# Moving one gate tile of layer 0 behind its queries, and dealing out the filler beside its attention

## The chip, the cores and the metric

The kernel runs on one core of one Trainium2 chip. The metric is device time in microseconds (us) of one launch. Before the change three runs took 1505.15, 1508.58 and 1509.13 us, a median of 1508.58 us. The engines are called by their names in the profile: PE multiplies matrices, ACT, DVE and POOL work on vectors, SP issues most of the transfers. Each engine takes its instructions strictly in the order of its own queue.

## What is computed

Two layers of a backbone over 512 latent tokens and 256 context tokens, 1024 channels wide, in float32. Of a layer only this matters here:

```python
h = modulate(rmsnorm(x, norm1_g[l]), shift, scale)        # shift, scale, gates: silu(cond) @ w_mod[l] + b_mod[l]
z = h @ w_in[l]                                           # columns: q 512 | k 128 | v 128 | u 512 | g 512
attn = softmax(rope(rmsnorm(q)) @ rope(rmsnorm(k)).T) @ v # context sees context, latent sees all 768 keys
gm = gelu(u) * (w_s @ group_layernorm(gelu(g)) + b_s)     # 4 groups of 128 channels, 128x128 position mixing
x = x + gate1 * (concat(attn, gm) @ w_out[l])
x = x + gate2 * (square(relu(modulate(rmsnorm(x, norm2_g[l])) @ w_ff1[l])) @ w_ff2[l])
```

## The kernel before

**Precision.** A product in float32 precision is three matmuls: every operand is kept as a rounded part `hi` and a rest `lo`, and hi\*hi, hi\*lo and lo\*hi are summed in PSUM. A weight block of 128x1024 is loaded by SP into one of two `raw` buffers; ACT casts it to `hi` and DVE or POOL subtracts to get `lo` (`split`, L206 to L208). Blocks of `w_mod` are loaded as they are, two to a place, and multiply in plain float32. All of them pass through a ring of four places (`hi` and `lo`, `RING = 4`), filled in the order of `block_order` (L120) and freed when the last matmul that reads a block is done.

**Projection of layer 0 (L764 to L783).** `PLAN` lists the pieces in order. `kv`, `A0` to `A2` and `B0` to `B2` are banks: 256 tokens by 256 columns, 48 matmuls of 256 columns into a PSUM buffer `pb` (two of them). A bank of A or B is two groups of `g`: it goes through gelu, the layer norm on DVE, the mixing matmuls with `w_s`, and then POOL multiplies the gate tile by it (L760). `u0` to `u3`, in the table `u2`, `u3` and the split pieces `w0`, `x0`, `w1`, `x1`, are the gate tiles: 128 channels of `u` by 768 tokens, for a whole tile two halves of 24 matmuls of 384 columns into a buffer `pa` (two of them), each half followed by ACT, DVE, ACT, DVE for gelu (`gelu2`, L690). The gate tile is written to `U` (tiles `C0`, `C1`), and the mixing of its group multiplies it in place. Behind the plan come the queries (L779 to L783): two groups of 256 columns by three banks of 256 tokens. DVE normalizes and turns a bank of queries (`qk`, L604), ACT and POOL split it (`stack`, L628), PE transposes it (`turn`, L636).

**Attention of layer 0 (L832 to L915).** There are 48 tiles of 128 queries of one head: 16 of the context (256 keys), then 32 of the latent tokens (768 keys). A tile is two products with the keys into `pa`, a row maximum on DVE (L842), an exponential on ACT (L845), transposes of the probabilities on PE (L861) with a copy on ACT and a subtraction on DVE (L863, L864), and for two tiles together the product with the values (L882 and before). Behind every tile `Flow.step` takes one piece of other work for PE, a filler, from a list.

**Fillers of layer 0.** First come four pieces of `w_mod` (letter m below; a piece is four float32 matmuls of 512 columns that use 32 columns of the array), then the string `FILL0` mixes 16 pieces `o` (one block row of `w_out` times the gMLP half of the mix, 12 matmuls of 384 columns) with 12 pieces m, then 8 pieces of the context's attention half of `w_out`, 12 matmuls of 256 columns each. `make_gm` (L786), which runs ahead of the first `o`, splits the four finished groups of `U` into `hi` and `lo`: ACT casts (L791), DVE subtracts for groups 0 and 1, POOL for groups 2 and 3 (L792). All four are needed within the first piece `o`.

**Order.** The program text gives an order, with a virtual clock (`fl.vt`) that puts off the later halves of a tile; the scheduler of the tile framework then sets the order on each engine. The rows in fences below are taken from that order. A name such as `pa_2029` is a buffer of the pool `pa`; `S` is the silu of the conditions, `A_39` to `A_46` the input `h`.

Of the kernel before, what the change touches and what calls it, by code (L numbers as in the profile page):

```python
# [12 lines left out]
ALU = mybir.AluOpType  # L13
# [14 lines left out]
PK1 = {"c": (0, 8), "cc": (8, 16), "bmod": (16, 112), "ng": (112, 144), "gn": (144, 152), "ident": (152, 280), "sel": (280, 312)}  # L28
PK2 = {"qg": (0, 64), "kg": (64, 128), "bs": (128, 640)}

PAR = {"KF": 1, "XO": 1, "MS": 3, "KB": 6, "S0": 200.0, "S2": 1.0, "BK": 1, "CS": 0, "S1": 2400.0, "NS": 2, "CX": 0,
# [14 lines left out]
class Flow:  # L48
# [59 lines left out]
    def run_fillers(self):  # L108
# [2 lines left out]

FILL0 = "oooooooomomomomomomomomommmm"
EARLY = [f"A{i}" for i in range(7, 3, -1)] + [f"B{i}" for i in range(7)] + ["C0", "C1"] + [f"A{i}" for i in range(7, 3, -1)]
PLAN = (("w0", "w1", "x0", "kv", "A0", "u2", "A1", "A2", "u3", "x1", "B0", "B1", "B2"),
        ("u0", "u3", "A0", "A1", "kv", "u1", "u2", "B0", "B1"))


def block_order():  # L120
# [3 lines left out]
    for l in range(DEPTH):  # L124
# [4 lines left out]
        for s in PLAN[l]:  # L129
            if s[0] in "uw":  # L130
                o.append(("u", l, int(s[1])))
            elif s in ("A0", "B0"):
                o += tok(l, 3 if s == "A0" else 4)
        o += tok(l, 1) + tok(l, 2)
        if l == 0:
            o += mod(4) + mod(5)
            rest = mod(6) + mod(7) + mod(8) + mod(9) + mod(10) + mod(11)
            n = 0
            for c in FILL0:
                if c == "m":  # L140
                    o.append(rest.pop(0))
                else:
                    if n % 4 == 0:
                        o.append(("out", 0, 0, n // 4))
                    n += 1
            o += rest
        else:
            o += [("out", l, 0, nb) for nb in range(4)]
# [12 lines left out]
def trunk(ctx: ExitStack, tc: tile.TileContext, xT, pk1, pk2, rope, wsT, w_mod, w_tok, w_u, w_out, w_ff1, w_ff2, outT):  # L161
# [431 lines left out]
    def layer(l, h, nxt, K, kv=None, kv0=0):  # L593
# [120 lines left out]
        def u_tile(m):  # L714
            wb = take("u", l, m)
            ps = pb() if nd == 1 and m < 2 else pa()
            for i, (off, n) in enumerate(dense):
                fm_mms(ps[:, i * 512:i * 512 + n], w8(wb, h), off, n)
                if i == nd - 1:
                    release()  # L720
                fl.tick()
                gelu2(U[m // 2][:, m % 2, off:off + n], ps[:, i * 512:i * 512 + n], [128, n])

        mixes = []

        def sink_g(gp):
            def f(tp, ps):
# [16 lines left out]
                @once  # L744
                def mixing():
                    mx = pt((128, 2, 256))
                    for g in range(2):
                        for t in range(2):
                            c = slice(t * 256 + g * 128, t * 256 + g * 128 + 128)
                            w = slice((gp * 2 + g) * 128, (gp * 2 + g) * 128 + 128)  # L750
                            for i, (a, b) in enumerate(((0, 0), (0, 1), (1, 0))):
                                mm(mx[:, g, t * 128:t * 128 + 128], vg[:, a, c], ws[:, b, w], i == 0, i == 2, 128)
                    e = tsm([128, 2, 256])
                    for g in range(2):
                        G_ = gp * 2 + g
                        vec.scalar_tensor_tensor(out=e[:, g, :].rearrange("p (t q) -> p t q", t=2), in0=mx[:, g, :].rearrange("p (t q) -> p t q", t=2),
                                                 scalar=gnh[:, G_:G_ + 1], in1=P2("bs")[:, G_ * 128:G_ * 128 + 128].unsqueeze(1).broadcast_to([128, 2, 128]),
                                                 op0=ALU.mult, op1=ALU.add)
                    u = U[gp][:, :, tp * 256:tp * 256 + 256]
                    pool_e.tensor_tensor(out=u, in0=e, in1=u, op=ALU.mult)  # L760
                mixes.append(mixing)
                fl.defer(PAR["G%d" % l], mixing)
            return f
# [15 lines left out]
        with region('q%d' % l):  # L779
            for g in range(2):  # L780
                qp = TokProj(l, 1 + g, h, NP, sink_q(g))
                for tp in range(NP):
                    qp.bank(tp)  # L783

        GM = []

# [133 lines left out]

        def mixed(a, b):
            for c in FILL0:
                next(a if c == "o" else b)
                yield
            yield from a
            yield from b

# [252 lines left out]
```

## Time and profile before

| | |
|---|---|
| three runs | 1505.15, 1508.58, 1509.13 us |
| the profiled execution | 1511.25 us, of which the span from the first to the last instruction is 1509.5 us |
| mean granted clock of PE | 0.991 |
| busy share of the span | PE 97%, DVE 60%, ACT 42%, POOL 23% |
| layer 0, projection and queries | about 40 to 176.5 us of the span |
| layer 0, attention | about 176.5 to 348 us |

A group's row in the profile gives the line, the engine, the operation, what it writes and reads, its shape and count, then busy time and mean duration in ns, then the idle time of the engine in front of it and who ended that. A timeline row gives start and duration in us. Matmuls overlap, so PE's pace is read from the distance of starts or from the chain of waits, not from the mean duration of one.

### The profile page before, as it was taken

Reading aid. Unit: us, or ns where it says so; the run is one execution under the profiler, and the core shown is the slowest. Engines: PE = TensorE matmul, PEld = TensorE weight load, DVE = VectorE, ACT = ScalarE, POOL = GpSimd, SP = SyncE. Lnnn points to the kernel's source line nnn. Section 1 sums busy time; section 2 is a strip of 40 time slices with the busy share of each in tenths; the row PEclk is TensorE's granted clock in tenths of the full one; section 3 lists DMA queues with packets and bytes.
Section 4 is the critical chain, followed back from the end, with each engine's and each line's share of the span. In section 5 each row is a group of like instructions: output and inputs, shape, how many; then the busy total and the mean of one; then the engine's idle time right before and its main releaser. Section 6 shows DMA issues by size and latency. Waiting matters only on the chain.

```text
span 1509.5 us, 22333 instructions
## 1 busy us (share of the span) xinstructions
PE 1459.7 (97%) x8770; PEld 1288.2 (85%) x8770; DVE 903.9 (60%) x1667; ACT 640.4 (42%) x1078; POOL 342.6 (23%) x322
## 2 busy tenths in 40 slices
PE   6999799999999999999999999999999999999998
PEld 2899787797889899998989888997889888888887
DVE  5877967787755555444444436766887544444443
ACT  3543355674545353433334233536774333322221
POOL 0112421312045552322323213146212000000000
PEclk9999999999999999999999999999999999999999
DMA  9121344401234333333333311221001333333222
GB/s 364 64 71 57 112 168 170 140 1 43 63 109 134 118 112 126 112 125 100 126 111 126 106 49 57 84 84 58 29 1 56 112 98 98 98 98 98 97 94 75
DMA packets 49945, 148.80 MB, mean 99 GB/s; under 512 B 5424, under 2 KB 6832, under 8 KB 49840
## 3 DMA queue, kind: packets, MB, share of 16 engines
q1 hardware_dynamic: 49264, 146.46, 29.5%
q8 instruction: 69, 1.13, 0.3%
q10 hardware_dynamic: 576, 0.92, 0.2%
q14 instruction: 36, 0.29, 0.1%
HBM read 145.26 MB, written 2.10 MB: 98 GB/s over the span
## 4 chain that ended last, share of the span: by engine, by line
PE 83%; DVE 8%; ACT 2%; POOL 2%; DMA 2%; issue 2%; SPq 0%; POOLq 0%; ACTq 0%; DVEq 0%
PE pa L203 52%; PE pb L203 24%; PE pt L861 3%; PE pt L203 2%; PE pb L338 1%; DMA B<-in_w_mod 1%; DMA X<-in_xT 1%; PE pt L643 1%; POOL acc L444 1%; DMA A<-in_w_mod 1%; DVE A L478 1%; DVE s L482 1%; DVE X L801 1%; DVE B L978 1%; DVE lo L208 0%
## 5 line engine op out<-in xcount | busy, mean ns | idle before, releaser
L203 PE MATMUL pa<-A,hi 128*128 128x384 f32 (+2 forms) x1696 | 449.2, 347 | 1.6 <-ACT w L971 0.7
L207 ACT CAST hi<-raw 128x1024 fp32r<-128x1024 f32 x171 | 179.5, 1051 | 466.2 <-PE pa L203 383.3
L208 DVE TENSOR_TENSOR lo<-raw,hi 128x1024 fp32r<-128x1024 f32 x155 | 194.3, 1254 | 232.8 <-ACT hi L207 229.4
L203 PEld LDWEIGHTS pa<-A,hi 128*128 128x128 f32 x1696 | 304.4, 188 | 25.7 <-ACT w L971 2.0
L203 PE MATMUL pa<-A,lo 128*128 128x384 f32 (+2 forms) x848 | 293.5, 346 | 1.1 <-DVE lo L208 1.1
L203 PE MATMUL pa<-B,hi 128*128 128x512 f32 (+1 forms) x900 | 239.8, 355 | 3.6 <-DVE X L801 3.6
L382 POOL TENSOR_TENSOR C<-C,s 128x512 f32<-128x512 f32 x112 | 164.7, 1485 | 315.5 <-ACT s L381 273.5
L203 PEld LDWEIGHTS pa<-B,hi 128*128 128x128 f32 x900 | 158.7, 189 | 31.6 <-DVE X L801 5.9
L203 PEld LDWEIGHTS pa<-A,lo 128*128 128x128 f32 x848 | 159.4, 188 | 12.2 <-DVE lo L208 1.5
L801 DVE SCALAR_TENSOR_TENSOR X<-pa,modT,X 128x512 f32<-128x512 f32 x126 | 82.9, 660 | 142.9 <-PE pa L203 142.9
L203 PE MATMUL pb<-B,hi 128*128 128x512 f32 (+1 forms) x600 | 157.9, 351 | 3.9 <-DVE X L801 3.9
L203 PE MATMUL pa<-B,lo 128*128 128x512 f32 (+1 forms) x450 | 157.7, 355 | 0.0
L203 PE MATMUL pb<-hi,A 128*128 128x256 f32 x672 | 126.4, 285 | 0.0
L203 PEld LDWEIGHTS pb<-B,hi 128*128 128x128 f32 x600 | 104.9, 191 | 18.3 <-DVE X L801 5.1
L801 DVE SCALAR_TENSOR_TENSOR X<-pb,modT,X 128x512 f32<-128x512 f32 (+3 forms) x116 | 70.9, 618 | 82.3 <-PE pb L203 82.0
L203 PEld LDWEIGHTS pb<-hi,A 128*128 128x128 f32 x672 | 106.3, 191 | 0.2 <-PE pb L203 0.2
L203 PE MATMUL pb<-B,lo 128*128 128x512 f32 (+1 forms) x300 | 104.9, 350 | 0.0
L203 PE MATMUL pb<-lo,A 128*128 128x256 f32 x336 | 95.1, 283 | 0.0
L381 ACT ACTIVATE s<-k,silu 128x512 f32<-128x512 f32 x112 | 77.0, 716 | 42.0 <-DMA k<-in_w_mod 29.0
L203 PEld LDWEIGHTS pa<-B,lo 128*128 128x128 f32 x450 | 84.1, 189 | 11.4
L203 PE MATMUL pb<-A,hi 128*128 128x512 f32 (+2 forms) x288 | 82.5, 363 | 2.2 <-POOL A L792 2.1
L864 DVE TENSOR_TENSOR A<-pt,A 128x384 fp32r<-128x384 f32 (+1 forms) x144 | 73.0, 534 | 10.2 <-ACT A L863 8.8
(173 smaller groups left out, 2224.4 us busy)
## 6 DMA issues: line engine op xcount, KB each, us to landing
raw<-in_w_ff SPq DMA_DIRECT2D x128, 512.0 KB, 3.5
k<-in_w_mod SPq DMA_DIRECT2D x96, 256.0 KB, 3.1
raw<-in_w_tok SPq DMA_DIRECT2D x19, 512.0 KB, 3.5
raw<-in_w_out SPq DMA_DIRECT2D x16, 512.0 KB, 3.4
lo<-in_w_mod SPq DMA_DIRECT2D x16, 512.0 KB, 4.5
hi<-in_w_mod SPq DMA_DIRECT2D x16, 512.0 KB, 3.7
A<-in_w_mod SPq DMA_DIRECT2D x8, 512.0 KB, 9.7
raw<-in_w_u SPq DMA_DIRECT2D x8, 512.0 KB, 3.4
```

Source lines behind the costliest of these rows:

```text
L203: pe.matmul(out, a, b, start=start, stop=stop)
L207: act.copy(hi, src)
L208: (eng or vec).tensor_tensor(out=lo, in0=src, in1=hi.bitcast(F32), op=ALU.subtract)
L338: pe.matmul(ps[q:q + 32, :], S32[:, k, :], ws_[k2 // 2][:, k2 % 2 * 512:(k2 % 2 + 1) * 512], start=k < ns, stop=k >= KT - ns)
L381: act.activation(p, w, AF.Copy, scale=s)
L382: pool_e.tensor_tensor(out=a, in0=a, in1=p, op=ALU.add)
L444: eng.tensor_tensor(out=self.acc, in0=self.acc, in1=sq, op=ALU.add)
L478: (pool_e if k % 2 < PAR['LP'].get('%d%d%d' % (l, w, off // 256), 0) else vec).scalar_tensor_tensor(out=h[k][:, 1, off:off + n], in0=t, sc ...
L482: vec.scalar_tensor_tensor(out=t, in0=xk(k)[:, off:off + n], scalar=Amod[l][w][:, k, cond:cond + 1], in1=self.bc[:, 0:n], op0=ALU.mult, op ...
L801: vec.scalar_tensor_tensor(out=xs, in0=src[:, s - off:e - off], scalar=modT[l][:, i * 8 + m, cond:cond + 1], in1=xs, op0=ALU.mult, op1=ALU ...
L861: pe.transpose(tp_[:, (kt - k0) * 128:(kt - k0) * 128 + 128], p[:, kt * 128:kt * 128 + 128], ident)
L864: vec.tensor_tensor(out=ptl[:, k0:k0 + step, d], in0=src, in1=pth[:, k0:k0 + step, d].bitcast(F32), op=ALU.subtract)
```

## The change

Layer 0's gate tile 3 is taken out of `PLAN` and multiplied behind the last bank of the queries (`LATE`, `u_tile`); its weight block moves in `block_order` to behind the two blocks of each group of queries. The mixing of group 3 now runs ahead of it: DVE writes the mixed values of that group straight into `U`, POOL multiplies only the other group of the pair, and when the tile is there, gelu writes to a scratch tile and POOL multiplies `U` by that, in two halves of 384 columns (new line 731). `FILL0` begins with two pieces m instead of the `o`s, has five dots, and the generator answers a dot with "wait": behind that tile of attention there is no filler. The 16 `o` and 12 `m` stay. Layer 1 has `LATE` None and stays as it is. Behind the change line numbers are 5 to 19 higher.

```diff
--- before.py
+++ after.py
@@ -28,6 +28,9 @@
 PK1 = {"c": (0, 8), "cc": (8, 16), "bmod": (16, 112), "ng": (112, 144), "gn": (144, 152), "ident": (152, 280), "sel": (280, 312)}
 PK2 = {"qg": (0, 64), "kg": (64, 128), "bs": (128, 640)}
 
+LATE = (3, None)
 
 
 PAR = {"KF": 1, "XO": 1, "MS": 3, "KB": 6, "S0": 200.0, "S2": 1.0, "BK": 1, "CS": 0, "S1": 2400.0, "NS": 2, "CX": 0,
@@ -111,9 +114,9 @@
 
 
 
-FILL0 = "oooooooomomomomomomomomommmm"
+FILL0 = "mmoooooooomomom.mom.mom.mom.mo.oo"
 EARLY = [f"A{i}" for i in range(7, 3, -1)] + [f"B{i}" for i in range(7)] + ["C0", "C1"] + [f"A{i}" for i in range(7, 3, -1)]
-PLAN = (("w0", "w1", "x0", "kv", "A0", "u2", "A1", "A2", "u3", "x1", "B0", "B1", "B2"),
+PLAN = (("w0", "w1", "x0", "kv", "A0", "u2", "A1", "A2", "x1", "B0", "B1", "B2"),
         ("u0", "u3", "A0", "A1", "kv", "u1", "u2", "B0", "B1"))
 
 
@@ -132,6 +135,8 @@
             elif s in ("A0", "B0"):
                 o += tok(l, 3 if s == "A0" else 4)
         o += tok(l, 1) + tok(l, 2)
+        if LATE[l] is not None:
+            o.append(("u", l, LATE[l]))
         if l == 0:
             o += mod(4) + mod(5)
             rest = mod(6) + mod(7) + mod(8) + mod(9) + mod(10) + mod(11)
@@ -139,7 +144,7 @@
             for c in FILL0:
                 if c == "m":
                     o.append(rest.pop(0))
-                else:
+                elif c == "o":
                     if n % 4 == 0:
                         o.append(("out", 0, 0, n // 4))
                     n += 1
@@ -719,7 +724,13 @@
                 if i == nd - 1:
                     release()
                 fl.tick()
-                gelu2(U[m // 2][:, m % 2, off:off + n], ps[:, i * 512:i * 512 + n], [128, n])
+                u, src = U[m // 2][:, m % 2, off:off + n], ps[:, i * 512:i * 512 + n]
+                if m == LATE[l]:
+                    v = gelu2(None, src, [128, n])
+                    pool_e.tensor_tensor(out=u, in0=v, in1=u, op=ALU.mult)
+                else:
+                    gelu2(u, src, [128, n])
 
         mixes = []
 
@@ -750,14 +761,17 @@
                             w = slice((gp * 2 + g) * 128, (gp * 2 + g) * 128 + 128)
                             for i, (a, b) in enumerate(((0, 0), (0, 1), (1, 0))):
                                 mm(mx[:, g, t * 128:t * 128 + 128], vg[:, a, c], ws[:, b, w], i == 0, i == 2, 128)
+                    u = U[gp][:, :, tp * 256:tp * 256 + 256]
                     e = tsm([128, 2, 256])
                     for g in range(2):
                         G_ = gp * 2 + g
-                        vec.scalar_tensor_tensor(out=e[:, g, :].rearrange("p (t q) -> p t q", t=2), in0=mx[:, g, :].rearrange("p (t q) -> p t q", t=2),
+                        to = u if G_ == LATE[l] else e
+                        vec.scalar_tensor_tensor(out=to[:, g, :].rearrange("p (t q) -> p t q", t=2), in0=mx[:, g, :].rearrange("p (t q) -> p t q", t=2),
                                                  scalar=gnh[:, G_:G_ + 1], in1=P2("bs")[:, G_ * 128:G_ * 128 + 128].unsqueeze(1).broadcast_to([128, 2, 128]),
                                                  op0=ALU.mult, op1=ALU.add)
-                    u = U[gp][:, :, tp * 256:tp * 256 + 256]
-                    pool_e.tensor_tensor(out=u, in0=e, in1=u, op=ALU.mult)
+                    gs = [g for g in range(2) if gp * 2 + g != LATE[l]]
+                    gs = slice(gs[0], gs[-1] + 1)
+                    pool_e.tensor_tensor(out=u[:, gs], in0=e[:, gs], in1=u[:, gs], op=ALU.mult)
                 mixes.append(mixing)
                 fl.defer(PAR["G%d" % l], mixing)
             return f
@@ -781,6 +795,8 @@
                 qp = TokProj(l, 1 + g, h, NP, sink_q(g))
                 for tp in range(NP):
                     qp.bank(tp)
+            if LATE[l] is not None:
+                u_tile(LATE[l])
 
         GM = []
 
@@ -920,8 +936,11 @@
 
         def mixed(a, b):
             for c in FILL0:
-                next(a if c == "o" else b)
-                yield
+                if c == ".":
+                    yield "wait"
+                else:
+                    next(a if c == "o" else b)
+                    yield
             yield from a
             yield from b
 

```

PE at the end of the queries. Before, the last bank of queries (`pb_2008`) is followed by the first tile's products (`pa_2092`), the first pieces of `w_mod` (L338, into `pb_2104` and `pb_2185`) and the transposes of queries (L643):

```order
L203 MATMUL pa_2092<-B_108_493,B_249_1617 128x256
L338 MATMUL pb_2104<-hi_1859,S_88 32x512 x2
L338 MATMUL pb_2104<-lo_1860,S_88 32x512 x2
L643 MATMUL pt_2109<-c_70,k_2045 128x128 x4
L643 MATMUL pt_2115<-c_70,k_2045 128x128 x4
L203 MATMUL pa_2128<-B_107_492,B_249_1617 128x256
L203 MATMUL pa_2128<-B_108_493,B_249_1617 128x256
L338 MATMUL pb_2104<-hi_1863,S_88 32x512 x2
L338 MATMUL pb_2104<-lo_1864,S_88 32x512 x2
L338 MATMUL pb_2185<-hi_2146,S_88 32x512 x2
L338 MATMUL pb_2185<-lo_2147,S_88 32x512 x2
```

Now half of gate tile 3 (`pa_2029`) stands between the last bank and those; here is the end of that half and what follows, down to the start of the other half:

```order
L208 MATMUL pa_2029<-A_46_178,hi_1796 128x384 x2
L208 MATMUL pa_2029<-A_46_178,lo_1797 128x384
L648 MATMUL pt_2054<-c_70,k_1982 128x128 x4
L648 MATMUL pt_2060<-c_70,k_1982 128x128 x4
L208 MATMUL pa_2125<-B_107_492,B_243_1552 128x256
L208 MATMUL pa_2125<-B_108_493,B_243_1552 128x256
L343 MATMUL pb_2137<-hi_1800,S_88 32x512 x2
L343 MATMUL pb_2137<-lo_1801,S_88 32x512 x2
L343 MATMUL pb_2137<-hi_2066,S_88 32x512
L648 MATMUL pt_2107<-c_70,k_2074 128x128 x2
L208 MATMUL pa_2029<-A_39_171,hi_1796 128x384 x2
```

What moved: the 48 matmuls of the gate tile now stand in front of the first and the second tile of attention, the second half of them behind transposes that read `k_2074`, which POOL writes.

DVE at the same place. Before, the subtractions of `make_gm` (L792) stand between two banks of queries, ahead of the operations that read the last bank `pb_2008` (L610 reads ACT's square of it):

```order
L297 SCALAR_TENSOR_TENSOR m_1995<-m_1997,m_1995 128x8
L625 TENSOR_TENSOR w_1988<-w_1988,m_1995 128x512
L792 TENSOR_TENSOR A_381_2274<-C_124_571,A_381_2274 128x768
L792 TENSOR_TENSOR A_382_2277<-C_124_571,A_382_2277 128x768
L610 TENSOR_REDUCE m_2074<-s_2072 128x8
L622 TENSOR_TENSOR w_2076<-pb_2008,k_33_148 128x512
```

Now the last bank is done (L630 is what was L625) when gelu of the gate tile comes (L698, L702 on `pa_2029`), the first tile's maximum (L858) among it, and `make_gm` (L808) stands behind the first half:

```order
L630 TENSOR_TENSOR w_2013<-w_2013,m_2016 128x512
L698 SCALAR_TENSOR_TENSOR s_2077<-s_2077,pa_2029 128x384
L582 TENSOR_SCALAR k_982_4820<-k_982_4820 128x64 x2
L592 TENSOR_SCALAR k_982_4820<-k_982_4820 128x512
L858 TENSOR_REDUCE m_2128<-pa_2125 128x1
L702 SCALAR_TENSOR_TENSOR s_2077<-s_2077,pa_2029 128x384
L863 RECIPROCAL m_2133<-m_2131 128x1
L808 TENSOR_TENSOR A_407_2358<-C_124_571,A_407_2358 128x768
L808 TENSOR_TENSOR A_408_2361<-C_124_571,A_408_2361 128x768
L698 SCALAR_TENSOR_TENSOR s_2119<-s_2119,pa_2029 128x384
L858 TENSOR_REDUCE m_2155<-pa_2152 128x1
L351 STREAM_TRANSPOSE s_2168<-pb_2137 128x512
```

What moved: `make_gm` on DVE went from ahead of the last bank of queries to behind it, and from then on maxima of attention tiles alternate with the gate tile's gelu.

POOL at the same place. Before, `make_gm` (L792) and the `lo` parts of two blocks of `w_out` stand in one run:

```order
L631 TENSOR_TENSOR k_2045<-w_1900,k_2045 128x8x64
L792 TENSOR_TENSOR A_383_2280<-C_125_572,A_383_2280 128x768
L792 TENSOR_TENSOR A_384_2283<-C_125_572,A_384_2283 128x768
L208 TENSOR_TENSOR lo_2157<-raw_2154,hi_2156 128x1024
L208 TENSOR_TENSOR lo_2163<-raw_2160,hi_2162 128x1024
L631 TENSOR_TENSOR k_2166<-w_1988,k_2166 128x8x64
L850 COPY rc_2102<-m_2100 128x64
```

Now the two multiplies of the gate tile (L731) are there, and `make_gm` for the last group (`A_410`) stands behind both blocks of `w_out` and four copies of the attention tiles' reciprocals (L866):

```order
L636 TENSOR_TENSOR k_2074<-w_1925,k_2074 128x8x64
L731 TENSOR_TENSOR C_125_572<-s_2077,C_125_572 128x384
L866 COPY rc_2135<-m_2133 128x64
L808 TENSOR_TENSOR A_409_2364<-C_125_572,A_409_2364 128x768
L636 TENSOR_TENSOR k_2142<-w_2013,k_2142 128x8x64
L731 TENSOR_TENSOR C_125_572<-s_2119,C_125_572 128x384
L866 COPY rc_2162<-m_2160 128x64
L213 TENSOR_TENSOR lo_2248<-raw_2245,hi_2247 128x1024
L866 COPY rc_2135<-m_2183 128x64
L213 TENSOR_TENSOR lo_2254<-raw_2251,hi_2253 128x1024
L866 COPY rc_2162<-m_2224 128x64
L808 TENSOR_TENSOR A_410_2367<-C_125_572,A_410_2367 128x768
```

What moved: the last operand that the first piece `o` needs is now written at the end of this run, not at its start.

## Prediction

> **What bounds the kernel now.** The page comes first: how much of the span each engine is busy.
>
> ```profile
> span 1509.5 us, 22333 instructions
> PE 1459.7 (97%) x8770; PEld 1288.2 (85%) x8770; DVE 903.9 (60%) x1667; ACT 640.4 (42%) x1078; POOL 342.6 (23%) x322
> ```
>
> PE is the bound, and the change takes no matmul away. It can gain only where PE stands or runs slowly, so the next view is the table of busy time by stretch, laid over layer 0 from the first banks of `g` to the end of attention (columns: stretch, its length, busy time of PE, weight loads, DVE, ACT, POOL with counts, granted clock, DMA share, GB/s).
>
> ```profile
> 97.00:145.00 48.00, 47.63 (x379) 47.49 (x379) 38.66 (x137) 17.15 (x26) 10.36 (x8) 1.00 0.22 67
> 145.00:176.50 31.50, 31.09 (x261) 30.71 (x261) 28.96 (x84) 10.89 (x19) 9.22 (x7) 1.00 0.21 69
> 176.50:195.50 19.00, 10.52 (x62) 4.00 (x62) 16.29 (x26) 6.58 (x14) 11.30 (x7) 0.73 0.56 198
> 230.00:290.00 60.00, 59.91 (x442) 46.70 (x440) 45.54 (x102) 35.77 (x79) 11.56 (x20) 1.00 0.49 167
> 290.00:324.00 34.00, 32.67 (x264) 31.11 (x261) 27.61 (x58) 23.11 (x53) 10.55 (x17) 1.00 0.10 32
> 324.00:348.00 24.00, 20.81 (x137) 18.12 (x136) 19.36 (x43) 17.36 (x41) 1.89 (x8) 0.93 0.00 1
> ```
>
> Two stretches fall out, with clocks of 0.73 and 0.93: the end of the queries (176.5 to 195.5) and the last tiles of attention (324 to 348). In the first, the timeline of PE shows the stop, and a finer table of stretches the clock behind it.
>
> ```profile
> 176.77 0.62 PE L338 MATMUL pb<-hi,S 128*32 128x512 f32 x2
> 177.77 1.09 PE L643 MATMUL pt<-c,k 128*128 128x128 f32 x8
> 178.62 0.48 PE L203 MATMUL pa<-B,B 128*128 128x256 f32 x2
> 179.49 0.60 PE L338 MATMUL pb<-lo,S 128*32 128x512 f32 x2
> 187.94 1.07 PE L338 MATMUL pb<-hi,S 128*32 128x512 f32 x2 [7.85 <-DVE w L622]
> 188.80 1.07 PE L338 MATMUL pb<-hi,S 128*32 128x512 f32 x2
> 188.00:192.00 4.00, 4.00 (x13) 1.00 (x14) 3.33 (x14) 1.07 (x3) 1.19 (x1) 0.50 0.31 84
> ```
>
> PE waits 7.85 us for a `pb` buffer that DVE has not read, and then works at a clock of 0.50. DVE's and POOL's timelines say why.
>
> ```profile
> 178.38 2.28 DVE L625 TENSOR_TENSOR w<-w,m 128x512 f32<-128x512 f32 x1
> 180.59 6.11 DVE L792 TENSOR_TENSOR A<-C,A 128x768 fp32r<-128x768 f32 x2
> 187.21 0.68 DVE L622 TENSOR_TENSOR w<-pb,k 128x512 f32<-128x512 f32 x1
> 176.50 3.61 POOL L792 TENSOR_TENSOR A<-C,A 128x768 fp32r<-128x768 f32 x2 [1.48 <-ACT A L791]
> 180.08 5.80 POOL L208 TENSOR_TENSOR lo<-raw,hi 128x1024 fp32r<-128x1024 f32 x2
> ```
>
> The read of the last bank (L622) stands behind two operations of `make_gm` of 3.05 us each.
>
> **Prices.** From the chain of waits, 24 matmuls of 384 columns (half of the gate tile), 36 of 256 and 24 of 512; then groups from the projection's stretch, the queries' and the last tiles'.
>
> ```profile
> 110.49 4.43 PE pa L203 x24
> 97.11 4.38 PE pb L203 x36
> 1192.45 5.44 PE pa L203 x24
> L693 DVE SCALAR_TENSOR_TENSOR s<-s,pa 128x384 f32<-128x384 f32 x2 | 1.1, 534 | 0.0
> L697 DVE SCALAR_TENSOR_TENSOR C<-s,pa 128x384 f32<-128x384 f32 x2 | 1.1, 546 | 0.0
> L692 ACT ACTIVATE s<-pa 128x384 f32<-128x384 f32 x2 | 1.0, 486 | 2.0 <-PE pa L203 2.0
> L630 ACT CAST k<-w 128x512 fp32r<-128x512 f32 x4 | 2.5, 627 | 7.1 <-DVE w L625 7.1
> L644 ACT CAST B<-pt 128x512 fp32r<-128x512 f32 x6 | 3.3, 590 | 4.5 <-PE pt L643 4.5
> L631 POOL TENSOR_TENSOR k<-w,k 128x512 fp32r<-128x512 f32 x4 | 5.4, 1339 | 13.0 <-ACT k L630 13.0
> L608 ACT ACTIVATE s<-pb 128x512 f32<-128x512 f32 x4 | 2.4, 597 | 7.4 <-PE pb L203 7.4
> L610 DVE TENSOR_REDUCE m<-s 128x8 f32<-128x512 f32 x5 | 3.4, 680 | 1.2 <-ACT s L608 1.2
> L614 DVE TENSOR_TENSOR w<-pb,G 128x512 f32<-128x512 f32 x4 | 2.7, 680 | 0.0
> L618 DVE TENSOR_TENSOR s<-pb,G 128x256 f32<-128x256 f32 x8 | 3.0, 413 | 0.0
> raw<-in_w_u SPq DMA_DIRECT2D x8, 512.0 KB, 3.4
> hi<-in_w_mod SPq DMA_DIRECT2D x5, 512.0 KB, 4.6
> L203 PE MATMUL pb<-A,B 128*128 128x256 f32 x49 | 9.8, 326 | 0.2 <-ACT A L863 0.2
> L861 PE MATMUL pt<-c,w 128*128 128x128 f32 x54 | 9.3, 293 | 2.8 <-DVE A L864 2.8
> L203 PE MATMUL pa<-B,B 128*128 128x512 f32 x14 | 5.3, 438 | 0.2 <-ACT w L845 0.2
> L203 PE MATMUL pa<-B,B 128*128 128x256 f32 x14 | 2.8, 281 | 0.0
> PE pt L861 <- DVE A L864: 2.8, 6, 1.3
> ```
>
> So a 256-column matmul costs 0.122 us, one of 512 columns 0.227; eight transposes take 178.62 - 177.77 = 0.85, 0.106 each; a float32 matmul of a piece m is 0.25 at full clock (four between the starts at 176.77 and 177.77). The moved tile is 2 x 4.43 = 8.9 us of PE.
>
> **Part A, the end of the queries.** What PE does in 176.5 to 195.5 would take at full clock 4 x 1.0 (four groups of L338) + 0.85 + 8 x 0.122 (four tiles' products) + 4 x 0.106 and some 0.3 of small ones = 6.5 us. 19.0 - 6.5 = 12.5 us are lost there. The change takes the cause away: `make_gm` on DVE is behind the last bank, and the tile's 8.9 us stand where PE stood. What is late next, counted from T, the end of the last bank of queries:
>
> First, `pt_2107`, in front of the tile's second half, needs `k_2074` from POOL. PE reaches it at T + 4.43 + 0.85 + 0.24 + 5 x 0.25 = 6.8. ACT casts for it behind the square of the first half and two casts of transposed queries: the transposes end at T + 5.3, then 2 x 0.59 + 0.63, then POOL 1.34, T + 8.4. PE waits 1.6.
>
> Second, there are now six pieces m behind the first six tiles instead of four, each two loads of 512 KB, and the gate tile's block holds one of four places till its last matmul, at T + 12.8. The piece loaded into that place (`hi_2186`) lands 4.6 later by the row above, T + 17.4; PE reaches it after six transposes, two products, seven matmuls of m and two transposes, 2.9 us on: T + 15.7. PE waits 1.7.
>
> Third, maxima of the first tiles stand behind gelu and `make_gm` on DVE, and the first piece `o` behind POOL's last part of `make_gm`. The bounds are 0, if all is covered, and 6.1, if `make_gm` stops PE for the 6.11 that it takes now; I take 2.2, nearer to the low end, since these maxima no longer hold a `pb` buffer. Together PE loses 5.5 us, between 3.3 and 9.4. Gain A: 12.5 - 5.5 = 7.0 us.
>
> At which clock would those waits leave PE? The row 290:324 holds one wait, and keeps 1.00; the row 324:348 shows 0.93 with six waits on one subtraction. Waits of 1.6 and 1.7 us, 8 us apart, are nearer to the first: no charge, and 24 x 0.07 = 1.7 us as the other bound. The Trainium skill (TensorE: Matmul & The Clock Gate, Part 1) says that the clock is halved after an idle window of about 3.4 us and restored after a busy one; the stretch at 0.50 behind a wait of 7.85 us agrees, and by that rule the charge would be 0.
>
> POOL gets two more reads of SBUF right there, beside DVE's L808. The Trainium skill (SBUF — State Buffer, Who interferes with whom) states that GpSimd reading SBUF and a DVE operation with two SBUF inputs exclude each other for a whole instruction, which speaks against this place; L625's 2.28 us while POOL's L792 runs agree, against 0.68 of L622 at the same width when POOL is done. By it only L808 would pay, the maxima and L880, with one SBUF input at most, would not, and the third wait above would be about 1 us smaller.
>
> **Part B, the projection.** Without the tile PE has 79.5 - 8.9 = 70.6 us of work from 97 to 176.5. DVE was busy 38.66 + 28.96 = 67.6; the tile's gelu, 2 x (0.53 + 0.55) = 2.2, goes, so 65.4 remain: 93% of PE's time instead of 85%. DVE idled 11.9 us in them, and 5.2 are left. Bounds: 0, if its two PSUM buffers absorb it, and 6.7, if it idles as much as before. PE idled 0.37 + 0.41 = 0.8 us in these stretches so far, so I take 1.0, with 4, nearer to the low bound, as the upper end. The tile's block is loaded behind the queries' four on SP, in 3.4 us, and its cast and subtraction move into the queries' stretch; three banks still lie between them and T, which hides both, and a load that came late would stop PE at T for what it lacks.
>
> **Part C, the attention tiles.** Before, 4 + 28 + 8 pieces stand behind the first 40 of 48 tiles, and the last eight have none. Work in 324 to 348: 49 x 0.122 + 54 x 0.106 + 14 x 0.227 + 14 x 0.122 for the same products' 256 columns + about 0.9 of small rows = 17.5 us, so 6.5 of the 24.0 are lost, 0.8 a tile. Now 4 + 33 + 8 = 45 tiles pass through the list, five of them by a dot. Five bare tiles at the end get work: 5 x 0.8 = 4.1 us. Five earlier tiles go bare; between filled neighbours such a tile costs between 0 and 0.8, and I take 0.3, as 230 to 290 runs with DVE at 76%. Gain C: 4.1 - 1.5 = 2.6, between 0 and 4.1. The last tile's own tail, with most of the low clock, stays.
>
> **Sum.** The tile's 8.9 us leave one stretch and come back in another: 0. Then -7.0 + 1.0 - 2.6 = -8.6 us. The span of 1509.5 becomes 1500.9. The profiled execution took 1511.25, 1.75 outside its span, and is 2.67 above the median of the runs, 1508.58; against that median the forecast is 1508.58 - 8.6 = 1500.0 us. The ends: -9.2 - 4.1 = -13.3, 1495.3; and -3.1 + 4 + 1.7 = +2.6, 1511.2.
>
> **Rivals.**
>
> 1. *The wait moves instead of going.* `A_410`, which the first `o` needs, now stands on POOL behind two blocks of `w_out` and four copies of attention tiles, and PE takes nothing past that `o`. If POOL comes 5 us after PE there, part A keeps 2.0, and the sum is -2.0 + 1.0 - 2.6 = -3.6: 1505.0. For it: POOL's L208 took 2.90 us each beside DVE. Against: six m, six tiles and 8.9 us stand in front.
> 2. *DVE becomes the bound of the projection.* All its 11.9 us of idling stay: 65.4 + 11.9 = 77.3 against 70.6, +6.7 us; the same lag reaches gelu and the first tiles, so that A's waits are 5.5 + 6.7 = 12.2 and its gain 0.3, and C's dots meet a DVE with no slack: 0. Sum +6.4: 1515.0, slower. It decides once DVE is more than about 3 us behind a finished bank (the next bank takes PE 48 x 0.122 = 5.9 us, and reading one takes 0.60 + 0.68 + 0.68 + 2 x 0.41 = 2.8). For it: 93% busy. Against: PE idled only 0.8 us in 79.5.
> 3. *Bare tiles are DVE's anyway.* Five dots cost 0.8 each, and fillers at the end only share PE's wait: C is +1.5 to +4.1. With 4.1: -7.0 + 1.0 + 4.1 = -1.9: 1506.7.
> 4. That the change does not do what it says is ruled out: the orders show the tile, `make_gm` and the pieces in their new places.
>
> **Chances.** About 0.3%, 4.5 us, can be told from no change, so faster means under 1504.1. Forecast 0.72 (nearly all of it faster), rival 1 0.14 (a fifth of it faster, the rest the same), rival 2 0.07 (slower), rival 3 0.07 (the same). Faster 0.73, same 0.20, slower 0.07. The range keeps the forecast's low end, rounded to 1495.0, and goes up to 1507.0, past rivals 1 and 3.
>
> **What would show it.** Right: behind the last bank no wait of PE over 3 us, a clock of 1.00 or nearly through T + 20, short waits on POOL's L636 and on a load of `w_mod`; the projection shorter by 8 us or more up to T; the bare stretch at the end of attention reduced to three tiles. Wrong: PE waiting for DVE inside the banks of `g` and the queries; a wait of over 5 us at the first `o` on POOL's L808; waits on L880 at the dots.

## The result, and the profile after

The changed kernel takes 1500.0 us (median of 6 runs, 1498.95 to 1502.22), and the kernel before beside it 1508.86 (6 runs): a ratio of 0.995, with a 95% interval of 0.9939 to 0.996 (the two medians alone divide to 0.994). The profiled execution took 1502.22 us, with a span of 1500.4, 9.1 shorter than before's. First the page's head, then the table by stretch, cut at the same places of the program as for before: the last bank of queries now ends at 168.7 instead of 176.4, and the last eight tiles of attention fill 316 to 340 instead of 324 to 348. The last row runs from that bank to the first matmul of the latent out-projection.

```profile
span 1500.4 us, 22327 instructions
```

```profile
97.00:145.00 48.00, 47.17 (x398) 47.00 (x398) 41.67 (x153) 15.58 (x24) 12.31 (x10) 1.00 0.19 62
145.00:168.70 23.70, 23.70 (x202) 23.70 (x201) 21.52 (x65) 8.36 (x15) 6.04 (x5) 1.00 0.21 70
168.70:195.50 26.80, 24.82 (x163) 15.74 (x162) 14.94 (x44) 16.36 (x37) 13.90 (x13) 1.00 0.73 254
316.00:340.00 24.00, 22.10 (x172) 20.51 (x170) 19.19 (x44) 17.28 (x42) 3.82 (x10) 1.00 0.01 2
168.70:340.20 171.50, 167.57 (x1174) 136.97 (x1173) 123.90 (x294) 106.53 (x245) 42.42 (x68) 1.00 0.36 124
```

Both bad clocks are gone: 0.73 and 0.93 have become 1.00. In the projection DVE is busy 41.67 + 21.52 = 63.2 of 71.7 us, and PE misses 0.8, as before. The last row has a counterpart in before:

```profile
176.40:347.80 171.40, 158.31 (x1126) 130.13 (x1125) 130.73 (x292) 102.20 (x239) 42.17 (x66) 0.96 0.34 118
```

Both take 171.4 or 171.5 us, but after has the gate tile in it (48 matmuls, 1174 against 1126), which starts at 168.71 and takes 4.17 us for its first half of 24 matmuls, from the first to the next instruction: 8.3 us for both at that pace. So attention gained 8.2 us and the projection lost nothing by giving the tile away. The waits of PE from 160 to 345 (what waited, for whom: sum, times, longest):

```profile
PE pt L877 <- DVE A L880: 1.3, 2, 1.0
PE pa L208 <- DVE s L702: 0.8, 1, 0.8
PE pb L343 <- DVE s L351: 0.6, 1, 0.6
PE pb L208 <- ACT A L879: 0.6, 2, 0.4
PE pt L648 <- POOL k L636: 0.5, 1, 0.5
```

The wait of 7.85 us has gone, none over 1.0 is left. There is no row for a load, and none for L808 of `make_gm`. The second and the last row stand around the gate tile's second half, in PE's timeline:

```profile
176.50 0.44 PE L648 MATMUL pt<-c,k 128*128 128x128 f32 x2 [0.52 <-POOL k L636]
177.79 0.62 PE L208 MATMUL pa<-A,hi 128*128 128x384 f32 x2 [0.84 <-DVE s L702]
```

The waits come to 3.8 us, and yet more is lost. The next table is worked out from PE's timeline: the distance between the starts of two neighbouring matmuls, less what it is at full speed (0.109 us at 128 columns, 0.120, 0.174 and 0.227 at 256, 384 and 512, some 0.03 at 8; 1.0 for a piece m). The last eight tiles are taken as the last 24 us. The last three columns are experiments.

| PE time lost, us | before | after | tile_alone | list_alone | whole |
|---|---|---|---|---|---|
| from 97 us to the last bank's end | 1.5 | 1.2 | 1.2 | 1.5 | 1.1 |
| from there to the first latent tile | 14.7 | 8.2 | 7.8 | 14.1 | 5.6 |
| latent tiles, to the out-projection | 13.0 | 11.3 | 11.5 | 11.1 | 6.6 |
| of these, the last eight tiles | 7.1 | 3.1 | 5.7 | 2.9 | 2.8 |

The last eight tiles gained 4.0 us, the 5 x 0.8 of the prediction. Of these, 1.4 are not the list's: tile_alone has before's list, and lost 5.7 there at a clock of 1.00 where before lost 7.1 at 0.93. And the latent tiles together gained only 1.7: something took 2.3 back. PE's timeline shows it, around three visits to pieces m:

```profile
232.63 0.62 PE L343 MATMUL pb<-hi,S 128*32 128x512 f32 x2
232.64 0.62 PE L343 MATMUL pb<-lo,S 128*32 128x512 f32 x2
233.08 0.60 PE L343 MATMUL pb<-hi,S 128*32 128x512 f32 x2
233.09 0.60 PE L343 MATMUL pb<-lo,S 128*32 128x512 f32 x2
233.62 0.88 PE L877 MATMUL pt<-c,w 128*128 128x128 f32 x6
...
235.13 1.04 PE L343 MATMUL pb<-hi,S 128*32 128x512 f32 x2
236.10 0.55 PE L877 MATMUL pt<-c,w 128*128 128x128 f32 x3
236.41 0.94 PE L208 MATMUL pa<-B,B 128*128 128x512 f32 x4
237.28 0.62 PE L343 MATMUL pb<-hi,S 128*32 128x512 f32 x1
...
238.27 0.39 PE L208 MATMUL pb<-A,B 128*128 128x256 f32 x1
```

The four matmuls of a piece (two records each, on four groups of 32 columns) that stand together run at the same time: from 232.63 to 233.62, 0.99 us for all eight records. Where the scheduler puts a transpose behind the first of them, that one alone takes 0.97 (235.13 to 236.10) and the other three 0.99 (237.28 to 238.27). A torn piece costs 1.96 us instead of 0.99. Counted in such steps of about 1 us, with at most four matmuls each, the 16 pieces take 19 steps in the order of before and of tile_alone, 24 in that of after, and 16 if none is torn; the expectations below say 18 where the traces have 19. The Trainium skill (TensorE: Matmul & The Clock Gate, Part 3: Packing small matmuls) says that matmuls placed on different 32-column tiles run concurrently; the trace agrees, and shows what one other instruction between them costs.

### The profile page after: what moved, and what is told of

Read it like the earlier page. It is cut to its first block, busy times and chain, and to the rows that moved or that the text cites. A ratio compares the mean times of both kernels' runs of the same rounds, so it can differ in the third digit from the quotient of the medians.

```text
span 1500.4 us, 22327 instructions
## 1 busy us (share of the span) xinstructions
PE 1460.4 (97%) x8770; PEld 1286.8 (86%) x8770; DVE 893.1 (60%) x1667; ACT 640.1 (43%) x1078; POOL 340.4 (23%) x324
## 4 chain that ended last, share of the span: by engine, by line
PE 88%; DVE 4%; DMA 2%; POOL 2%; ACT 2%; issue 1%; SPq 0%; POOLq 0%; ACTq 0%; DVEq 0%
PE pa L208 52%; PE pb L208 27%; PE pt L877 3%; PE pt L208 2%; PE pb L343 1%; PE pt L648 1%; DMA raw<-in_w_tok 1%; DMA B<-in_w_mod 1%; POOL acc L449 1%; DMA A<-in_w_mod 1%; DVE A L483 1%; DVE s L487 1%; DVE X L817 1%; POOL m L289 0%; DVE B L997 0%
## 5 line engine op out<-in xcount | busy, mean ns | idle before, releaser
L208 PE MATMUL pb<-lo,A 128*128 128x256 f32 x336 | 95.1, 283 | 0.0
L208 PEld LDWEIGHTS pa<-B,lo 128*128 128x128 f32 x450 | 84.0, 188 | 11.3
```

The costliest lines, as they stand in the source:

```text
L208: pe.matmul(out, a, b, start=start, stop=stop)
```

## The experiments

Twelve kernels in three groups; those of a group and the kernel before ran on one chip. "Stretch" is from the end of the last bank of queries to the first matmul of the latent out-projection in the profiled execution; where the gate tile is not in it, 8.3 is to be added for comparison.

| kernel | median, us | before beside it | ratio, 95% interval | stretch, us |
|---|---|---|---|---|
| tile_alone | 1503.22 | 1507.55 | 0.9972, 0.996 to 0.9985 | 171.4 |
| list_alone | 1508.52 | 1507.55 | 1.0006, 0.9998 to 1.0015 | 168.8 + 8.3 |
| whole | 1496.56 | 1507.55 | 0.9928, 0.9915 to 0.9941 | 164.2 |
| gm_behind | 1508.82 | 1507.55 | 1.0007, 0.9997 to 1.0016 | 168.5 + 8.3 |
| after_again | 1500.37 | 1507.67 | 0.9944, 0.9928 to 0.9961 | 173.5 |
| whole_no_dots | 1496.73 | 1507.67 | 0.9918, 0.9905 to 0.9932 | 166.4 |
| dots8 | 1493.62 | 1507.67 | 0.99, 0.9885 to 0.9915 | 164.8 |
| gm_behind_dve | 1504.36 | 1507.67 | 0.9976, 0.9967 to 0.9985 | 166.9 + 8.3 |
| consts_later | 1499.34 | 1506.39 | 0.9958, 0.9944 to 0.9973 | 170.3 |
| best | 1490.90 | 1506.39 | 0.9896, 0.9882 to 0.991 | 161.0 |
| best_b | 1493.00 | 1506.39 | 0.9914, 0.99 to 0.9928 | 165.4 |
| no_tile_best | 1497.58 | 1506.39 | 0.9944, 0.9931 to 0.9957 | 158.5 + 8.3 |

Two theories of the result: that of the prediction (the tile fills PE's stop behind the last bank, the dealt-out list fills the tail), and that of torn pieces (the tile does that, and what the list gains at the tail is paid back in pieces that it tears).

### One part of the change alone

**tile_alone**: the late tile with before's list.

```diff
-FILL0 = "mmoooooooomomom.mom.mom.mom.mo.oo"
+FILL0 = "oooooooomomomomomomomomommmm"
```

> The late gate tile, with the filler string of before. By the prediction's terms only part A and part B come: 1508.9 - 7.0 + 1.0 = 1502.9 us. By the theory of torn pieces (a piece m whose four matmuls stand together takes 1.0 us, one that other matmuls tear into 1 and 3 takes 0.98 + 0.99 = 1.97 us) this kernel keeps its pieces as whole as before did: its order has 18 runs of these matmuls, like before, where after has 24. Then nothing of the tile's gain is paid back: the wait and the half clock behind the last bank (12.5 us lost before, 3.2 us after besides pieces) go, the bare last tiles stay, and the time is about 1508.9 - 9 = 1500 us, no slower than the whole change although its list is missing.

**list_alone**: the new list with the tile in its old place.

```diff
-LATE = (3, None)
+LATE = (None, None)
-PLAN = (("w0", "w1", "x0", "kv", "A0", "u2", "A1", "A2", "x1", "B0", "B1", "B2"),
+PLAN = (("w0", "w1", "x0", "kv", "A0", "u2", "A1", "A2", "u3", "x1", "B0", "B1", "B2"),
```

> The filler string of after, with the gate tile where it was before. By the prediction's terms only part C comes: -2.6, 1506.3 us. By the theory of torn pieces the tail's 4.1 us are paid for by six more runs of piece matmuls (24 instead of 18) of about 0.98 us each, 5.9 us: 1508.9 - 4.1 + 5.9 = 1510.7 us, no faster than before. make_gm still stands ahead of the last bank of queries on DVE, so both expect the 7.85 us wait and the half clock to be there.

By time the tile alone brings 0.28%, 4.3 us, less than either theory expected; in the profile its stretch is as short as that of the whole change (171.4), and its span 1500.7. The list alone, between its two expectations, brings nothing that can be told from 0; in the profile its stretch is 2.5 us shorter than before's. So most of the change is the tile, and the list is worth far less than its tail. The 2.8 us by which tile_alone's median stands above the repeated changed kernel's are not in its stretch; nothing here shows where its other executions lost them. One place where they may: its last eight tiles keep before's six waits, which left the clock at 0.93 in before's profile and at 1.00 in its own. The waits, and the table of stretches:

```profile
PE pt L877 <- DVE A L880: 2.8, 6, 1.3
```

```profile
314.60:338.60 24.00, 20.79 (x148) 17.94 (x147) 20.77 (x45) 18.88 (x44) 1.90 (x8) 1.00 0.00 1
```

### Pieces kept whole

**whole**: the changed kernel; the last three matmuls of a piece are tied to the first and have priority.

```diff
+                with tc.high_priority() if j > 3 and k2 else nullcontext():
-                pe.matmul(ps[q:q + 32, :], ...)
+                    ins = pe.matmul(ps[q:q + 32, :], ...)
+                if j > 3 and k2:
+                    tc.add_manual_dep(ins.ins, head.ins.name, NoSync, reason="whole piece")
+                else:
+                    head = ins
```

> The changed kernel, with the four matmuls of each piece m kept next to each other in PE's order (the last three are tied behind the first and given priority). Nothing is left out. By the theory of torn pieces the 24 runs of after become 16 of 1.0 us: -7.8 us, 1492 us, and the trace shows no run of two records of these matmuls of 0.98 us. If a piece costs four times 0.25 us wherever its matmuls stand, as the prediction had it, the time stays at 1500 us.

The table of stretches, for the matmuls of pieces alone (stretch, length, PE busy with its count, weight loads, clock, DMA), of after, of tile_alone and of whole:

```profile
168.70:340.20 171.50, 25.13 (x128) 3.65 (x128) 1.00 0.36 124
```

```profile
167.20:338.60 171.40, 19.75 (x128) 3.09 (x128) 1.00 0.36 124
```

```profile
166.80:331.00 164.20, 16.84 (x128) 2.62 (x128) 1.00 0.37 129
```

The same 128 records take 8.3 us less, and the stretch is 7.3 us shorter: shown for the profiled executions. By time the gain against the changed kernel is 0.9928 to 0.9944 or 0.995, 2.4 to 3.3 us, with intervals that overlap, and the median is 4.6 us above the 1492 expected; only the profiled execution (1493.23 us) comes near it. The mean granted clock was 0.998 in that one, 0.994 or 0.995 in the other four (1494.66 to 1496.94 us). In tile_alone it is 0.998 in the shortest execution (1500.52) and 0.994 in the two longest (1504.58 and 1505.32). So time and clock go together; where in the kernel the clock fell is not seen in one profile.

**whole_no_dots** and **dots8** change only the string of that kernel.

```diff
-FILL0 = "mmoooooooomomom.mom.mom.mom.mo.oo"
+FILL0 = "mmoooooooomomommommommommooo"            # whole_no_dots
+FILL0 = "mmoooooooomomom.mom.mom.mom.mo.o.o.."    # dots8
```

> The kernel with whole pieces, and the five dots taken out of the filler string, so that the last eight tiles of attention are bare again. Whole pieces alone took 164.2 us from the last bank of queries to the latent out-projection. If bare tiles at the end cost 0.8 us each and those between filled ones nothing, it takes 4.1 us more: 168.3. By the prediction's 0.3 us for each dot it takes 2.6 us more: 166.8. If a bare tile costs the same wherever it stands (the third rival), 164.2.

> The kernel with whole pieces and three dots more, so that all 48 tiles of attention pass through the list and none is bare at the end but the last. Of whole pieces' 164.2 us, 2.8 us are lost in the last 23. If they are lost for want of work behind the last three tiles, some 2 us go, 162 us; if they belong to the last tile's own chain (product, maximum, exponential, transposes, product), nothing goes.

In whole_no_dots the last tiles show the same six waits again:

```profile
PE pt L882 <- DVE A L885: 2.8, 6, 1.3
```

Its stretch is 2.2 us longer than that of whole: between the prediction's 2.6 and the third rival's 0, much nearer to the first. That it is near 2.6 is luck in part: worked out as in the table above, whole_no_dots loses 5.7 us in the last eight tiles, 2.9 more than whole and not 4.1, so the five dots cost about 0.7 together and not 1.5. By time the two are equal, so the five dots' worth is shown by the profile only. dots8 has no wait for L885 from 300 us on, so the rest of the tail was want of work too and not the last tile's own chain; from the first latent tile on it takes 107.1 us against 108.9 of whole. Its whole stretch is 0.6 longer all the same, for the reason of the next experiment.

### What PE waits for at the gate tile's second half

DVE's timeline of after at that place:

```profile
173.66 0.55 DVE L698 SCALAR_TENSOR_TENSOR s<-s,pa 128x384 f32<-128x384 f32 x1 [0.22 <-ACT s L697]
176.23 0.37 DVE L582 TENSOR_SCALAR k<-k 128x64 f32<-128x64 f32 x2 [2.01 <-DMA k<-in_pk]
176.52 0.42 DVE L592 TENSOR_SCALAR k<-k 128x512 f32<-128x512 f32 x1
176.86 0.41 DVE L858 TENSOR_REDUCE m<-pa 128x1 f32<-128x256 f32 x1
177.19 0.54 DVE L702 SCALAR_TENSOR_TENSOR s<-s,pa 128x384 f32<-128x384 f32 x1
```

L582 scales the next layer's constants, which are still being loaded. DVE stands for 2.01 us, and the first tile's maximum (L858) and gelu's last read (L702) stand behind it. **after_again** is the changed kernel once more.

> The changed kernel once more, as the mark for the others of this group: 0.995 of before, 1500 us. From the last bank of queries to the first matmul of the latent out-projection its trace had 171.5 us, the moved tile's 8.3 us in them; this stretch holds less of what varies between executions than the whole span, and the others of this group are compared by it.

Its time is the same, but its stretch is 2.0 us longer. PE's timeline at the gate tile's second half:

```profile
174.19 0.44 PE L648 MATMUL pt<-c,k 128*128 128x128 f32 x2 [0.52 <-POOL k L636]
175.90 0.62 PE L208 MATMUL pa<-A,hi 128*128 128x384 f32 x2 [1.26 <-DVE s L702]
176.35 0.35 PE L208 MATMUL pa<-A,lo 128*128 128x384 f32 x1
...
177.20 0.84 PE L208 MATMUL pa<-A,hi 128*128 128x384 f32 x2
...
178.16 0.84 PE L208 MATMUL pa<-A,hi 128*128 128x384 f32 x2
...
180.72 0.51 PE L208 MATMUL pa<-A,hi 128*128 128x384 f32 x2
...
181.24 0.51 PE L208 MATMUL pa<-A,hi 128*128 128x384 f32 x2
```

Here the wait is 1.26 us instead of 0.84, and from about 177 to 180 three matmuls take 0.96 us (177.20 to 178.16) instead of 0.52 (180.72 to 181.24): the clock is halved. To the first latent tile it takes 58.7 us instead of 56.7, 0.4 by the wait and 1.6 by the clock. dots8 waited longer there, and paid the clock as well:

```profile
177.02 0.62 PE L208 MATMUL pa<-A,hi 128*128 128x384 f32 x2 [1.74 <-DVE s L707]
```

**consts_later** ties L582 and L592 behind the first latent tile's maximum.

```diff
-            vec.tensor_scalar_mul(g, g, s)
+            behind(l, vec.tensor_scalar_mul(g, g, s))
...
-        vec.tensor_scalar_mul(P2("bs"), P2("bs"), 0.5)
+        behind(l, vec.tensor_scalar_mul(P2("bs"), P2("bs"), 0.5))
```

> The changed kernel, with the three first operations on the next layer's constants (L582 twice, L592) tied on DVE behind the first latent tile's maximum. In after and its repetition DVE stands 2.01 and 2.51 us in front of L582 for a load that lands 5.4 and 5.8 us after its issue; the first tile's maximum and gelu's L702 are behind it, and PE waits 0.84 and 1.26 us for L702; behind the longer of these two waits the clock was halved (from the last bank to the first latent tile 58.7 us against 56.7). If that load is what PE waits for, the wait falls below 0.3 us, the clock there is 1.00, the stretch takes 55.5 to 56 us, and the time falls by 1 to 3 us against 1500.4. If PE is held there by the transposes' operand from POOL or by ACT's tanh, the wait stays at 0.8 us or more and the time does too.

Its PE at the same place:

```profile
174.31 0.44 PE L654 MATMUL pt<-c,k 128*128 128x128 f32 x2 [0.53 <-POOL k L642]
174.50 0.59 PE L208 MATMUL pa<-A,hi 128*128 128x384 f32 x2
174.93 0.34 PE L208 MATMUL pa<-A,lo 128*128 128x384 f32 x1
```

The wait is gone and the clock is full; the stretch to the first latent tile takes 55.5 us, as expected. The cause is shown. The time is not: 0.9958 against 0.9944 and 0.995 of the changed kernel is no gain that can be told.

### make_gm's place without the tile

**gm_behind**: before, with one edge in DVE's order.

```diff
+                if l == 0 and g < 2:
+                    tc.add_manual_dep(lo.ins, lastqk[l].ins.name, NoSync, reason="behind the last bank")
```

> Before, with one edge more: the two subtractions of make_gm on DVE are issued behind the last operation on the last bank of queries. No gate tile is moved, the filler string is that of before. If the 7.85 us wait came only from make_gm's place on DVE, PE waits about 2 us for the last bank to be read (180.6 us + 0.68 + 0.68, against PE at 179.7), the clock stays full, and the time falls by 8 to 9 us, to 1500 or 1501, as much as with the moved tile. If the tile is needed as work for PE there, the wait only moves to the next reader, and no more than 4 us are gained: 1505 us or more.

The second expectation holds, and more: nothing was gained. The timelines of PE, DVE and POOL say where the wait went:

```profile
187.14 0.69 PE L864 MATMUL pt<-c,w 128*128 128x128 f32 x2 [3.80 <-ACT w L848]
```

```profile
180.72 2.28 DVE L288 TENSOR_SCALAR m<-m 128x8 int32<-128x8 int32 x1
183.04 2.26 DVE L291 TENSOR_TENSOR m<-m 128x8 f32<-128x8 f32 x1
186.01 0.42 DVE L845 TENSOR_REDUCE m<-pa 128x1 f32<-128x256 f32 x1
```

```profile
180.62 4.65 POOL L209 TENSOR_TENSOR lo<-raw,hi 128x1024 fp32r<-128x1024 f32 x2
```

PE now stops for the first tile's exponential, 3.80 us. Its maximum on DVE (L845) stands behind two operations on eight elements a row that take 2.28 and 2.26 us: the second ends at 185.3, with POOL's pair of subtractions. **gm_behind_dve** gives those subtractions to DVE.

```diff
-"WP": ['out1', 'out0']
+"WP": ['out1']
```

> Before with make_gm behind the last bank of queries on DVE, and the subtractions of the blocks of w_out on DVE instead of POOL. With POOL's subtractions (2.3 us each) two operations on 128x8 elements of DVE's chain took 2.28 and 2.26 us instead of 0.17, PE then waited 3.8 us for the first tile's exponential behind them, and nothing was gained. If POOL's operations held DVE there, these two fall below 0.5 us, the wait shrinks to 1 us or less, the clock stays at 1.00, and the time falls by 4 us or more against that kernel, to 1504 us or below. If DVE is late by its own queue, the wait stays near 3.8 us and the time at 1508 us.

```profile
179.19 0.17 DVE L288 TENSOR_SCALAR m<-m 128x8 int32<-128x8 int32 x1
179.40 0.17 DVE L291 TENSOR_TENSOR m<-m 128x8 f32<-128x8 f32 x1
```

```profile
181.20 1.04 PE L339 MATMUL pb<-hi,S 128*32 128x512 f32 x2 [1.46 <-DMA hi<-in_w_mod]
183.54 0.69 PE L864 MATMUL pt<-c,w 128*128 128x128 f32 x2 [1.30 <-ACT w L848]
```

0.17 us each, a wait of 1.30 (ahead of it PE waits for a load once, 1.46), and 1504.36 us, 4.5 less than gm_behind and about the 1504 expected: POOL held DVE. Two of its expectations were missed, though: the wait is not 1 us or less, and the clock from 176.5 to 195.5 is 0.91, not 1.00. The Trainium skill (SBUF — State Buffer, Who interferes with whom) says that DVE and GpSimd (POOL) share a pair of ports, and that whoever issues first holds it for its whole instruction; these rows agree. L288 has one input in SBUF and L291 two; why the first was held as long as the second is not shown here.

### Everything together

**best**: dots8 with the constants later. **best_b**: two of its added dots among the context's tiles. **no_tile_best**: best with gate tile 3 back in `PLAN`, and the edits of gm_behind_dve.

```diff
-FILL0 = "mmoooooooomomom.mom.mom.mom.mo.o.o.."    # best
+FILL0 = "mmooo.ooo.oomomom.mom.mom.mom.mo.o.o"    # best_b
```

> Whole pieces, eight dots at the later places, and the next layer's constants behind the first latent tile: everything found so far. Without the last of these the stretch from the last bank to the first latent tile took 57.7 us, a wait of 1.74 us for L707 and 3.4 us at half clock among them; with it 54.5 us are expected, and a time of 1490.5 us, 3 us below 1493.6. If the load is not the cause, 1493.6.

> The kernel before this one, with two of the three added dots among the context's tiles instead of all three behind the last pieces m. If a bare tile costs nothing wherever it has filled neighbours, the time is the same within 1 us. If DVE and ACT are short of time among the context's first tiles, a bare tile there costs up to 0.8 us, 1.6 us in all.

> All the other edits without the moved gate tile: tile 3 in its place of before, whole pieces, eight dots, constants later, make_gm on DVE behind the last bank of queries, and w_out's subtractions on DVE. The scheduler leaves three pieces torn in two halves here, 3 us. If the tile is worth something as work for PE behind the last bank, the waits of make_gm_behind with the subtractions on DVE stay (1.46 us for a load, 1.30 us for an exponential, a clock of 0.91 in that stretch): 3 us more besides the pieces, so 1496 to 1497 us. If the tile only served to bring the order on DVE and POOL about, this kernel loses the pieces' 3 us alone: 1493 to 1494 us.

best takes 1490.9 us, 15.5 less than before beside it, against 1490.5 expected; its interval lies below the changed kernel's. Its way to the first latent tile takes 53.8 us, against 54.5 expected and 57.7 in dots8. The 2.7 us to dots8 in time are partly the chip: before takes 1.3 us less here, so against before 1.4 us are left, with intervals that overlap. best_b takes 2.1 us more than best, past both of its expectations (1 and 1.6 us), with intervals that just overlap. Its stretch is 4.4 us longer; a single wait for DVE among the latent tiles, 1.7 us, and a clock of 0.71 from 256 to 260 behind it, 1.2 us, are most of that, and the rest stays open:

```profile
PE pt L361 <- DVE m L876: 1.7, 1, 1.7
```

no_tile_best is 6.7 us slower than best, near what was expected if the tile is worth something as work: 3.3 are torn pieces (20.16 us for its 128 records of them, 16.84 in best), and up to the first latent tile PE waits for exponentials:

```profile
PE pt L893 <- ACT w L877: 3.0, 2, 2.6
```

In best PE waits 0.3 us for exponentials there. So the tile pays as work for PE, beyond the order that it brings about.

## Why the prediction was right, and where it was not

The sum was -8.6 us of span, and -9.1 came. The span of 1500.9 was forecast, and 1500.4 measured. The parts are less exact, and that they add up so well is luck in part: A gained 6.5 instead of 7.0, B lost nothing instead of 1.0, C gained 1.7 instead of 2.6, and the errors cancel.

**What bounds it.** Right: the stop behind the last bank and its clock were the place. But `make_gm` ahead of the last bank was only the first cause. gm_behind takes it away, and the wait moves to DVE's next operations, which POOL holds. The change gains there because the tile's products stand in front and POOL's subtractions for `w_out` come later (the first starts at 187.1). That POOL slows DVE at this place was read in the prediction from L625's 2.28 us against L622's 0.68, two operations with a different number of inputs in SBUF; the same operation in after, L630 at 172.75, took 0.69 with POOL idle, so the reading stands.

**Part A, gain 7.0.** 14.7 - 8.2 = 6.5 us in the first profile, and 2.0 less in the repeated one. Its three waits were wrong one by one. PE's wait for `k_2074` was 0.52 and not 1.6. The load of `hi_2186` is in no row of waits (1.7 expected). The third was 0.84 for gelu's L702, behind a load of constants: those rows, L582 and L592, stood in the order of DVE that the prediction had before it, and it gave them no price. In their place the torn pieces cost: six pieces from 168.7 to 195.5 took 9.3 us, 0.5 of waiting among them, instead of 6.0.

**The clock.** "No charge, and 1.7 as the other bound": one execution paid nothing, the repeated one 1.6. Both ends occur with the same order.

**Part B, a loss of 1.0.** None came: from the first to the last bank of the projection 103.7 us became 95.1, the tile's 8.3 and 0.3 more. DVE was busy 88% of these stretches (63.2 of 71.7 us), not 93%, and PE missed 0.8 us in them, as before.

**Part C, gain 2.6.** The last eight tiles gave 4.0, but 1.4 of them were the clock: the 0.8 us that a bare tile was said to lose came from a stretch at 0.93. At 1.00 the eight lose 5.7 (tile_alone), and the list's part is 2.6. The dots cost about 0.1 each where pieces are whole (2.9 - 2.2 = 0.7 for five), not 0.3. The step that failed is the price of a piece: "a float32 matmul of a piece m is 0.25 at full clock" holds for four that stand together, and the new list makes 24 steps of them where 16 would do. The pieces took 25.13 us instead of 16.84, and of C 1.7 was left in the latent tiles; beside the tile alone the list gained nothing (stretches of 171.5 and 171.4 us). "The last tile's own tail, with most of the low clock, stays" was wrong: the six waits became two, 1.3 us in all, and with three dots more these went too. The clock was 1.00, but in tile_alone it was so with all six waits, so its rise is not shown to be the list's.

**The rest.** 0.9 us were lost ahead of the banks, and 1.5 gained behind attention, where the change does nothing. The last bank ends between 166.4 and 168.7 us in the nine traces with the moved tile, and what lies behind attention took 1158.0 to 1163.0 us in the fourteen traces, so nothing is made of either.

**Rivals.** The first (a wait for `A_410` at the first `o`) has no row. The second (DVE as bound of the projection) is refuted by the projection's rows. The third (bare tiles are DVE's anyway) is refuted by the profiles of whole_no_dots and dots8.

## What to carry to other kernels

Work that is moved into a stop also brings an order with it; undo one without the other to learn which of them paid, and look at who is late next. Small matmuls that share the array by column groups have a price as a group: count in PE's order how often a group is torn when a list of fillers is changed. An operation that waits for a load belongs behind what the bound engine needs next, however small it is.

## What had not been expected of the hardware

A float32 matmul of 512 columns on a group of 32 array columns takes 0.97 us alone, and four of them together, on four groups, 0.99. Wherever a transpose or another product stood between them here, it cost a second run of 0.97 to 0.99.

DVE operations on 128x8 elements took 2.28 and 2.26 us while POOL subtracted 1024 columns a row, and 0.17 when it didn't.

Waits of 0.52 and 0.84 us, 1.3 us apart, left the clock at 1.00; 0.52 and 1.26 at the same place halved it a microsecond later for some 3 us. The Trainium skill (TensorE: Matmul & The Clock Gate, Part 1) speaks of an idle window of about 3.4 us, free-running; none of these waits was as long as that, so a window that is partly idle can be enough. The six waits in the last tiles, 2.8 us in all, lowered the clock to 0.93 in before and left it at 1.00 in tile_alone: the same waits can go either way.
